# Two mixers of an adaLN block rewritten: pooling with scale, gate, shift and bias folded in, state space with dt in the exponent and GpSimd left with the masks

## The chip, the cores and the metric

The kernel runs as one launch on one core of a Trainium2 chip. The metric is device microseconds (us) of an execution. A core has a matrix engine (TensorE, PE in the profile, with its weight loads as PEld), VectorE (DVE), ScalarE (ACT), GpSimd (POOL) and SyncE (SP), whose queue issues every DMA of this kernel. The engines run their own queues in order and wait for one another through semaphores.

## The reference, cut to what matters

Two model blocks run one after the other on x of 256 tokens by 1024 channels, in fp32. The first has two layers of FFN, token mixer (gated delta rule beside attention) and FFN; the change leaves it alone. The second has a layer with a state-space mixer and a layer with a pooling mixer, each between two FFNs; a vector c gives each of its steps a shift, scale and gate, sums over `ada_w`. The state-space mixer runs over 256 context tokens first and hands its final states to the 256 main tokens; it has 32 heads in 4 groups, two directions d, chunks of 128 tokens.

```python
# state space, per direction, chunk and head; a_cum = cumsum(dt * A)
xdt = x * dt
states = einsum(B, exp(a_last - a_cum), xdt)          # per chunk
h = h * exp(a_last) + states                          # over the chunks
Lmat = exp(where(mask, a_cum[l] - a_cum[s], -inf))
y_diag = einsum(C @ B.T, Lmat, xdt); y_off = C @ h_in * exp(a_cum)
y = d_skip * x + sum over d of (y_diag + y_off)
out = rmsnorm_per_group(y * silu(z)) @ w_out          # context: only h_final is kept

# pooling, 4 groups of 256 channels, windows 2, 4, 8, 16 on a 4 x 64 grid
u = rmsnorm(x) * (1 + sc) + sh
pooled[g] = mean_over_window(u[g]) - u[g]             # a fixed 256 x 256 matrix per group
x = x + gate * scale * (pooled @ w[g] + bias)
```

## The kernel before

Tokens lie in two tiles (t = 0, 1) of 128 rows. A weight stream feeds almost all of the program: a unit is one 512 KB DMA into a `raw` buffer (6 of them), a cast to a short fp32r part `hi` on ACT (L345), the rest `lo` on DVE (L346), and three fp32r matmuls for each product (`mm3`, L351 to L353). Some units ("whole", L384 and L411) keep fp32 and show two matmul instructions a product. `stream` runs units with the loads ahead; the last five units of a phase ("deep") keep their t = 1 matmuls back, so that PE has work while tile 0 is finished and normalised for the next phase. `tick` works on the `ada_w` sums in the background: a DMA into one of two `ad` buffers (L530), a DVE multiply-add (L540), matmuls. Intermediate tiles of 128 by 512 are pages, 38 of them; PSUM has 4 banks "ps" and 4 "mm". `merge(a, b, r)` writes two pieces of work alternately, and a scheduler that runs before the launch orders each engine's queue; SP's queue issues DMAs in that order and stops at one whose buffer is not free.

Around the change the program goes: the FFN pair (main and context tokens), `ssd_ctx`, `ssd_lat`, FFN, FFN, `pool_mix`, FFN, final norm.

`ssd_ctx` projects the context (four streams us[0..3], one a group); core(g) transposes the group's tokens (L1622), copies them to SBUF (L1716), multiplies by the decay to the chunk's end and dt on POOL (`ended`, L1689), multiplies with B on PE (L1723) and stores the states (L1728). core(0..2) run beside us[1..3]; core(3) runs after them, interleaved with `mid`, the norm of the main tokens (L683, L690, transposes L248, L702, split L723/724).

`ssd_lat` has a head (z, dt and the B and C projections, 17 units), then `shared` (with `stacks`, which brings a_cum into the form that the masks take), then four core(g), merged with the streams of the other groups' projections and z. In core(g) POOL makes 8 masked stacks (L1784), PE two products that give the exponent (L1827/1828), ACT takes Exp (L1830, W), W is multiplied by dt (L1832; d = 0 on DVE, d = 1 on POOL), DVE adds the two directions (L1844) and multiplies by C B^T (L1845), and PE applies W (`diagonal`, L1792). The off-diagonal part goes L1839 (PE), L1841 and L1842 (DVE). The skip term d_skip * x is POOL's (L1816). Then the gate, the norm (L1795 to L1800), and the output units.

`PoolPrep` norms x for the pooling mixer: `scaled` (L1908), shift added (L1913), the bias added to x on POOL (L1916), with `pool_b`, `pool_scale` and the pooling matrices `poolq` loaded in `a`. `pool_mix` pools all groups (L1940), splits the result into hi and lo (`split`, L254/255), multiplies with `pool_w` as streamed units, and adds acc * scale * gate to x (L1927/1928).

## Time and profile before

| what | value |
| --- | --- |
| median of 3 runs | 3037.53 us (3035.7 to 3040.81) |
| the profiled execution | 3034.64 us, span 3032.9 us |
| PE busy | 2899.7 us (96%) |
| DVE busy | 2226.4 us (73%) |
| ACT busy | 1343.6 us (44%) |
| POOL busy | 176.0 us (6%), 148 instructions |

The profile shows one execution. The span is the time from its first to its last recorded instruction; the execution's own time is 1.7 us longer. Of the view of stretches the reader takes each engine's busy time between two moments and the clock that PE was granted (1.00 is 2.4 GHz, half of it 1.2 GHz). The chain is the sequence of work that ended last, followed back from the end: what stands on it could have shortened the run, what doesn't lay beside it. The waits say what ended an engine's idle time.

### The profile page before, as it was taken

Reading aid. Unit: us, or ns where it says so; the run is one execution under the profiler, and the core shown is the slowest. Engines: PE = TensorE matmul, PEld = TensorE weight load, DVE = VectorE, ACT = ScalarE, POOL = GpSimd, SP = SyncE. Lnnn points to the kernel's source line nnn. Section 1 sums busy time; section 2 is a strip of 40 time slices with the busy share of each in tenths; the row PEclk is TensorE's granted clock in tenths of the full one; section 3 lists DMA queues with packets and bytes.
Section 4 is the critical chain, followed back from the end, with each engine's and each line's share of the span. In section 5 each row is a group of like instructions: output and inputs, shape, how many; then the busy total and the mean of one; then the engine's idle time right before and its main releaser. Section 6 shows DMA issues by size and latency. Waiting matters only on the chain.

```text
span 3032.9 us, 42634 instructions
## 1 busy us (share of the span) xinstructions
PE 2899.7 (96%) x16035; PEld 2429.6 (80%) x16035; DVE 2226.4 (73%) x4000; ACT 1343.6 (44%) x2110; POOL 176.0 (6%) x148
## 2 busy tenths in 40 slices
PE   7998999999999899999999999998989999998898
PEld 4988776779889797678898888886866798897697
DVE  6779757777677776677878655776799875888754
ACT  4544323554444443245545223454535544543443
POOL 1000110000000011000000000002044000001000
PEclk9999999999999999999999999999999999999899
DMA  8885534468778742245776545844523587788563
GB/s 279 288 287 174 169 100 121 131 203 265 248 243 288 258 150 79 85 143 160 232 232 210 154 148 168 298 159 136 170 79 126 180 278 239 231 295 284 167 186 134
DMA packets 275777, 589.56 MB, mean 194 GB/s; under 512 B 28759, under 2 KB 72933, under 8 KB 275571
## 3 DMA queue, kind: packets, MB, share of 16 engines
q1 hardware_dynamic: 275571, 586.84, 59.7%
q8 instruction: 126, 2.06, 0.3%
q14 instruction: 80, 0.66, 0.1%
HBM read 582.57 MB, written 4.19 MB: 193 GB/s over the span
## 4 chain that ended last, share of the span: by engine, by line
PE 73%; DVE 15%; DMA 5%; ACT 4%; issue 3%; POOL 0%; SPq 0%; DVEq 0%; ACTq 0%; POOLq 0%
PE mm L351 19%; PE mm L352 18%; PE mm L353 18%; PE mm L411 5%; PE mm L384 4%; DMA ad<-ada_w 3%; DVE lo L346 2%; PE ps L248 2%; DVE acc L540 2%; PE ps L1260 1%; ACT hi L345 1%; PE ps L558 1%; PE ps L1267 1%; DMA raw<-w_branch_a 1%; PE ps L1160 1%
## 5 line engine op out<-in xcount | busy, mean ns | idle before, releaser
L345 ACT CAST hi<-raw 128x1024 fp32r<-128x1024 f32 x591 | 615.7, 1044 | 875.0 <-PE mm L352 369.8
L346 DVE TENSOR_TENSOR lo<-raw,hi 128x1024 fp32r<-128x1024 f32 x591 | 714.2, 1217 | 302.4 <-ACT hi L345 290.4
L351 PE MATMUL mm<-hTa,lo 128*128 128x256 f32 (+1 forms) x2160 | 649.5, 301 | 14.0 <-DVE lo L346 9.6
L352 PE MATMUL mm<-hTa,hi 128*128 128x256 f32 (+1 forms) x2160 | 642.6, 298 | 0.0
L353 PE MATMUL mm<-hTa,hi 128*128 128x256 f32 x1872 | 530.6, 284 | 0.0
L351 PEld LDWEIGHTS mm<-hTa,lo 128*128 128x128 f32 x2160 | 413.0, 191 | 30.5 <-DVE lo L346 10.6
L352 PEld LDWEIGHTS mm<-hTa,hi 128*128 128x128 f32 x2160 | 413.3, 191 | 13.3 <-issue 1.4
L540 DVE SCALAR_TENSOR_TENSOR acc<-ad,cond,acc 128x1024 f32<-128x1024 f32 x238 | 308.6, 1297 | 87.1 <-DMA ad<-ada_w 85.0
L353 PEld LDWEIGHTS mm<-hTa,hi 128*128 128x128 f32 x1872 | 359.0, 192 | 0.0
L351 PE MATMUL mm<-hi,pg 128*128 128x512 f32 (+1 forms) x844 | 332.6, 394 | 0.4 <-DVE pg L2014 0.4
L352 PE MATMUL mm<-hi,pg 128*128 128x512 f32 (+1 forms) x844 | 328.6, 389 | 0.0
L353 PE MATMUL mm<-lo,pg 128*128 128x512 f32 (+1 forms) x844 | 327.6, 388 | 0.0
L351 PE MATMUL mm<-hi,hTa 128*128 128x512 f32 (+1 forms) x444 | 183.4, 413 | 25.7 <-DVE hTa L724 18.0
L411 PE MATMUL mm<-hTb,raw 128*128 128x256 f32 x896 | 205.8, 384 | 0.0
L411 PEld LDWEIGHTS mm<-hTb,raw 128*128 128x128 f32 x896 | 169.8, 193 | 27.5 <-issue 5.6
L351 PEld LDWEIGHTS mm<-hi,pg 128*128 128x128 f32 x844 | 158.6, 188 | 33.9 <-issue 1.7
L352 PE MATMUL mm<-hi,hTa 128*128 128x512 f32 (+1 forms) x468 | 185.1, 396 | 0.0
L352 PEld LDWEIGHTS mm<-hi,pg 128*128 128x128 f32 x844 | 158.7, 188 | 32.8 <-issue 2.2
L353 PEld LDWEIGHTS mm<-lo,pg 128*128 128x128 f32 x844 | 158.6, 188 | 32.8 <-issue 0.5
L353 PE MATMUL mm<-lo,hTa 128*128 128x512 f32 (+1 forms) x468 | 184.8, 396 | 0.0
L384 PE MATMUL mm<-raw,hTb 128*128 128x512 f32 x320 | 151.7, 605 | 0.0
L248 PEld LDWEIGHTS ps<-con,pg 128*128 128x128 f32 x748 | 87.6, 143 | 53.6 <-issue 29.6
(443 smaller groups left out, 4510.0 us busy)
## 6 DMA issues: line engine op xcount, KB each, us to landing
ad<-ada_w SPq DMA_DIRECT2D x272, 512.0 KB
raw<-ffn_w SPq DMA_DIRECT2D x264, 512.0 KB
raw<-ffn_w_down SPq DMA_DIRECT2D x110, 512.0 KB
raw<-w_in SPq DMA_DIRECT2D x104, 512.0 KB
raw<-ffn_w_gate SPq DMA_DIRECT2D x88, 512.0 KB
raw<-ffn_w_up SPq DMA_DIRECT2D x88, 512.0 KB
raw<-ssd_w_in SPq DMA_DIRECT2D x60, 512.0 KB
raw<-w_branch_a SPq DMA_DIRECT2D x16, 512.0 KB
```

The source lines that it names most:

```text
L248: T.transpose(o[:, sl], src[:, sl], ident)
L345: in_order("hi", ACT.copy(hi[:, 0:m], raw[:, 0:m]))
L346: in_order(lane, eng.tensor_sub(lo[:, 0:m], raw[:, 0:m], hi[:, 0:m]))
L351: T.matmul(o, sl, mh, start=first, stop=False)
L352: T.matmul(o, sh, mh, start=False, stop=False)
L353: T.matmul(o, sh, ml, start=False, stop=last)
L384: T.matmul(d[c0 // 512][:, 0:min(cw, c0 + 512) - c0], sf, wt[c0 // 512], start=k == 0, stop=k == kt - 1)
L411: T.matmul(acc[m][:, 0:S], wt[0][:, SL[m]], hT.whole[:, k, :], start=k == 0, stop=k == KD - 1)
L540: after_edge(V.scalar_tensor_tensor(out=o, in0=w, scalar=sc, in1=o, op0=ALU.mult, op1=ALU.add))
L558: T.matmul(q, ones, self.acc[i][h], start=True, stop=True)
L1160: T.matmul(qs[:, col:col + 1], sq[:, hh * S + t * P:hh * S + (t + 1) * P], ones[:, 0:1], start=True, stop=True)
L1260: T.matmul(blk(y[:, H2[h]]), M[t][:, sl], odd(Ub[t][:, sl]), start=True, stop=True)
```

## The change

State space. `stacks` forms log(dt) (floored at 1e-37, ACT's Ln) and an extra accumulating matmul with the identity subtracts it from one of the two exponents, so that Exp gives W already times dt; the multiplies of L1832 go, and hi, lo and the stacks have 512 columns of source instead of 256. `ended` moves from POOL to DVE. The skip term moves to DVE, which reads x straight from the transposes' PSUM bank. The last multiply of the norm moves from DVE to ACT. `ssd_ctx` runs the norm of the main tokens within g = 2 and returns core(3), which is merged with the head of `ssd_lat`.

Pooling. `PoolPrep.early` runs in the background of the FFN before: it loads the column sums of the pooling matrices (`poolc`), bias, scale, `pool_w` and `poolq`, and folds scale * gate into `pool_w` and the bias. The shift enters the pooled product as a product of one row (shift by column sums), the bias as a product with a row of ones; x is only scaled. The pooled result is copied once and multiplied in fp32, and x takes the sum from PSUM.

```diff
         def stacks(self, t):
-            rep_ = pg()
+            rep_, lg = pg(), small(64, tag="lg")
+            V.tensor_scalar(out=lg, in0=self.dt[t], scalar1=1e-37, scalar2=None, op0=ALU.max)
+            ACT.activation(lg, lg, AF.Ln)
             for d in range(2):
                 V.tensor_copy(rep_[:, d * P:(d + 1) * P].rearrange("p (n c) -> p n c", c=HS), bcm(self.dA[t][:, d * HS:(d + 1) * HS], 4))
+                V.tensor_scalar(out=rep_[:, S + d * P:S + (d + 1) * P].rearrange("p (n c) -> p n c", c=HS), in0=bcm(lg[:, d * HS:(d + 1) * HS], 4),
+                                scalar1=-1.0, scalar2=None, op0=ALU.mult)
             q = ps()
             for d in range(2):
-                T.matmul(q[:, d * P:(d + 1) * P], rep_[:, d * P:(d + 1) * P], C("le" if d == 0 else "ge"), start=True, stop=True)
-            hl, st = pg(R32), pg(R32)
-            hi, lo = hl[:, 0:S], hl[:, S:2 * S]
-            ACT.copy(hi, q[:, 0:S])
-            V.tensor_sub(lo, q[:, 0:S], hi)
+                ra, rl, tri = rep_[:, d * P:(d + 1) * P], rep_[:, S + d * P:S + (d + 1) * P], C("le" if d == 0 else "ge")
+                T.matmul(q[:, S + d * P:S + (d + 1) * P], ra, tri, start=True, stop=True)
+                T.matmul(q[:, d * P:(d + 1) * P], ra, tri, start=True, stop=False)
+                T.matmul(q[:, d * P:(d + 1) * P], rl, ident, start=False, stop=True)
+            hi, lo, st = pg(R32), pg(R32), pg(R32)
+            ACT.copy(hi, q)
+            V.tensor_sub(lo, q, hi)
             c = lambda n: C("quad")[:, n:n + 1]
-            for o, a in ((st[:, 0:S], 0), (st[:, S:2 * S], 3)):
-                V.tensor_scalar(out=o, in0=hi, scalar1=c(a), scalar2=c(a + 2), op0=ALU.mult, op1=ALU.add)
-                V.scalar_tensor_tensor(out=o, in0=lo, scalar=c(a + 1), in1=o, op0=ALU.mult, op1=ALU.add)
+            for sl_, a in ((slice(0, S), 0), (slice(S, 2 * S), 3)):
+                V.tensor_scalar(out=st[:, sl_], in0=hi[:, sl_], scalar1=c(a), scalar2=c(a + 2), op0=ALU.mult, op1=ALU.add)
+                V.scalar_tensor_tensor(out=st[:, sl_], in0=lo[:, sl_], scalar=c(a + 1), in1=st[:, sl_], op0=ALU.mult, op1=ALU.add)
             self.left[t] = [st[:, d * P:(d + 1) * P] for d in range(2)]
             self.right[t] = [st[:, S + d * P:S + (d + 1) * P] for d in range(2)]
...
             e = pg()
-            G.tensor_mul(h8(e), h8(xt), bc(self.dx[t][:, d * HS + g * 8:d * HS + g * 8 + 8], 64))
+            V.tensor_mul(h8(e), h8(xt), bc(self.dx[t][:, d * HS + g * 8:d * HS + g * 8 + 8], 64))
             return e
...
         run(us[0])
-        for g in range(4):
+        for g in range(3):
             c = core(g)
-            if g < 3:
-                advance(us[g + 1], CN)
-                merge(us[g + 1], c, CR)
-                run(c)
-            else:
-                for _ in c:
-                    next(mid, None)
+            advance(us[g + 1], CN)
+            if g == 2:
+                run(first_of(mid, NT))
+            merge(us[g + 1], c, CR)
+            run(c)
         run(mid)
+        return core(3)
+    left_over = [None]
...
-        run(stream(zs + dt.units + conv_units(hT, 4096, 16, BT) + conv_units(hT, 4608, 20, CT)))
+        head = stream(zs + dt.units + conv_units(hT, 4096, 16, BT) + conv_units(hT, 4608, 20, CT))
+        merge(head, left_over[0], 1.0)
+        run(left_over[0])
...
                 rsqrt(rs, ss, 1.0 / 512, EPS, 1)
-                V.tensor_scalar(out=yy, in0=yy, scalar1=rs, scalar2=None, op0=ALU.mult)
+                ACT.activation(yy, yy, AF.Copy, scale=rs)
...
-                xt[t] = pg()
-                ACT.copy(xt[t], to_tok(xT[g], t))
+                xt[t], y[g, t] = pg(), pg()
+                q = to_tok(xT[g], t)
+                ACT.copy(xt[t], q)
+                V.tensor_mul(h8(y[g, t]), h8(q), bc(sc_["dsk"][:, g * 8:g * 8 + 8], 64))
                 e[t] = pg()
                 V.tensor_mul(h8(e[t]), h8(xt[t]), bc(dt.dx[t][:, hd(t)], 64))
                 yield
             masked(0, 1)
-            for t in range(NT):
-                y[g, t] = pg()
-                G.tensor_mul(h8(y[g, t]), h8(xt[t]), bc(sc_["dsk"][:, g * 8:g * 8 + 8], 64))
...
-                    h0 = d * HS + g * 8 + i * 4
-                    (G if d else V).tensor_mul(h4(W[t, i, d]), h4(W[t, i, d]), bc(dt.dt[t][:, h0:h0 + 4]))
...
     class PoolPrep(Prep):
...
+        def early(self):
+            for _ in range(4):
+                yield
+            self.q, self.w = [], []
+            self.sums, self.bias = pg(), pg()
+            for h in range(2):
+                load(self.sums[32 * h:32 * h + 1, :].rearrange("p (g l) -> p g l", l=S), A["poolc"][2 * h:2 * h + 2, :].unsqueeze(0))
+                load(self.bias[32 * h:32 * h + 1, :], A["pool_b_2"][0, 2 * h:2 * h + 2, :].rearrange("g d -> (g d)").unsqueeze(0))
+            for g in range(4):
+                self.w.append(pg())
+                load(self.w[g].rearrange("p (k d) -> p k d", k=2), A["pool_w_2"][0, g].rearrange("(k p) d -> p k d", p=P))
+            yield
+            for h in range(2):
+                psc = pg()
+                load(psc, A["pool_scale_2"][0, h * 512:(h + 1) * 512].partition_broadcast(P))
+                yield
+                V.tensor_mul(psc, psc, self.m.has("gate", 0)[:, h * 512:(h + 1) * 512])
+                V.tensor_mul(self.bias[32 * h:32 * h + 1, :], self.bias[32 * h:32 * h + 1, :], psc[32 * h:32 * h + 1, :])
+                yield
+                for g in (2 * h, 2 * h + 1):
+                    w_ = self.w[g].rearrange("p (k d) -> p k d", k=2)
+                    V.tensor_mul(w_, w_, bcm(psc[:, g % 2 * S:g % 2 * S + S], 2))
+                    yield
+            for g in range(4):
+                self.q.append(pg())
+                load(self.q[g].rearrange("p (t l) -> p t l", t=NT), A["poolq"][g].rearrange("(t p) l -> p t l", p=P))
+            yield
         def scaled(self, t, h, src, r):
-            V.scalar_tensor_tensor(out=self.xn[t, h], in0=src, scalar=r, in1=self.m.has("sc", 0)[h], op0=ALU.mult, op1=ALU.mult)
+            ins = V.scalar_tensor_tensor(out=self.xn[t, h], in0=src, scalar=r, in1=self.m.has("sc", 0)[h], op0=ALU.mult, op1=ALU.mult)
+            edge[0] = ins.ins
         def b(self, t):
-            for h in range(2):
-                u = self.xn.pop((t, h))
-                edge[0] = V.tensor_add(u, u, self.m.has("sh", 0)[h]).ins
-                self.xn["u", t, h] = u
-            for h in range(2):
-                G.tensor_add(x(t, h), x(t, h), self.rows[h][0])
+            pass
     def pool_mix(prep, m, nxt):
         yield ()
         flush()
-        u = prep.xn
+        u, sh = prep.xn, m.has("sh", 0)
         acc = Lazy(2)
...
+        row = lambda ap, h: ap[32 * h:32 * h + 1]
+        pooled, qs = [], [[(mmb if g > 1 else ps)() for _ in range(2)] for g in range(4)]
+        def pool(g, t):
             for c in range(2):
                 k = g * 2 + c
-                for t in range(NT):
-                    T.matmul(q[:, c * S:(c + 1) * S], u["u", t, k // 4][:, SL[k % 4]], qv[:, t, :], start=t == 0, stop=t == NT - 1)
-            pooled[g] = split(q)
-            us += tok_units(lambda k, t, g=g: tuple(a[:, k * S + t * P:k * S + (t + 1) * P] for a in pooled[g]), A["pool_w_2"][0, g],
-                            lambda t, g=g: [acc[t][g // 2][:, (g % 2) * S:(g % 2 + 1) * S]], (lambda t, g=g: ended(t, g // 2)) if g % 2 else None)
-        run(stream(seam(us, False)))
+                o = qs[g][c][:, 0:S]
+                if t == 0:
+                    T.matmul(o, row(sh[k // 4], k // 4)[:, SL[k % 4]], row(prep.sums, k // 4)[:, g % 2 * S:g % 2 * S + S], start=True, stop=False)
+                T.matmul(o, u[t, k // 4][:, SL[k % 4]], prep.q[g][:, t * S:t * S + S], start=False, stop=t == NT - 1)
+        for t in range(NT):
+            for g in range(4):
+                pool(g, t)
+                if t:
+                    p_ = pg()
+                    pooled.append(p_)
+                    ACT.copy(p_[:, 0:S], qs[g][0][:, 0:S])
+                    V.tensor_copy(p_[:, S:], qs[g][1][:, 0:S])
+        for t in range(NT):
+            for h in range(2):
+                o = acc[t][h]
+                T.matmul(o, row(ones, h), row(prep.bias, h), start=True, stop=False)
+                for g in (2 * h, 2 * h + 1):
+                    for k in range(2):
+                        T.matmul(o[:, g % 2 * S:g % 2 * S + S], pooled[g][:, k * S + t * P:k * S + (t + 1) * P], prep.w[g][:, k * S:k * S + S], start=False, stop=g % 2 + k == 2)
+                V.tensor_add(x(t, h), x(t, h), o)
+            nxt.a(t)
+        for t in range(NT):
+            nxt.b(t)
+        yield
...
-        mid = ahead(p0) if i + 1 == PAIR else ()
+        mid = ahead(p0) if i + 1 == PAIR else nxt.early() if keys[i + 1:i + 2] == [(1, 1, 1)] else ()
...
-            ssd_ctx(p1, ahead(preps[LAT]))
+            left_over[0] = ssd_ctx(p1, ahead(preps[LAT]))
...
+    arrays["poolc"] = POOLQ.sum(1)
```

POOL in the state-space core, group 0, before (L1784 masks, L1816 skip term, L1832 W times dt):

```order
L1784 TENSOR_TENSOR pg_20123<-pg_20064,con 128x512
L1784 TENSOR_TENSOR pg_20125<-pg_20064,con 128x512
L1784 TENSOR_TENSOR pg_20159<-pg_20064,con 128x512
L1784 TENSOR_TENSOR pg_20161<-pg_20064,con 128x512
L1816 TENSOR_TENSOR pg_20163<-pg_20131,sdsk 128x512
L1816 TENSOR_TENSOR pg_20165<-pg_20140,sdsk 128x512
L1784 TENSOR_TENSOR pg_20231<-pg_20092,con 128x512
L1784 TENSOR_TENSOR pg_20233<-pg_20092,con 128x512
L1832 TENSOR_TENSOR pg_20228<-pg_20228,pg_19581 128x512
L1784 TENSOR_TENSOR pg_20254<-pg_20092,con 128x512
L1784 TENSOR_TENSOR pg_20256<-pg_20092,con 128x512
L1832 TENSOR_TENSOR pg_20251<-pg_20251,pg_19581 128x512
```

and after (L1793 masks):

```order
L1793 TENSOR_TENSOR pg_20143<-pg_20074,con 128x512
L1793 TENSOR_TENSOR pg_20145<-pg_20074,con 128x512
L1793 TENSOR_TENSOR pg_20183<-pg_20074,con 128x512
L1793 TENSOR_TENSOR pg_20185<-pg_20074,con 128x512
L1793 TENSOR_TENSOR pg_20249<-pg_20112,con 128x512
L1793 TENSOR_TENSOR pg_20251<-pg_20112,con 128x512
L1793 TENSOR_TENSOR pg_20270<-pg_20112,con 128x512
L1793 TENSOR_TENSOR pg_20272<-pg_20112,con 128x512
```

Between the masks nothing is left.

PE where `ssd_ctx` ends and the head of `ssd_lat` begins, before (L1622 transposes of x, L1723 states, L248 transposes of the norm, L351 to L353 the head's first units):

```order
L1622 MATMUL ps_19238<-con,pg_19171 128x128 x2
L1622 MATMUL ps_19238<-con,pg_19191 128x128 x2
L1622 MATMUL ps_19267<-con,pg_19171 128x128 x2
L1622 MATMUL ps_19267<-con,pg_19191 128x128 x2
L1723 MATMUL ps_19297<-pg_19295,pg_18903 128x512
L1723 MATMUL ps_19301<-pg_19299,pg_18910 128x512
L1723 MATMUL ps_19311<-pg_19309,pg_18903 128x512
L248 MATMUL ps_19315<-con,pg_19246 128x128 x4
L248 MATMUL ps_19326<-con,pg_19248 128x128 x4
L1723 MATMUL ps_19339<-pg_19337,pg_18910 128x512
L248 MATMUL ps_19341<-con,pg_19275 128x128 x4
L248 MATMUL ps_19352<-con,pg_19277 128x128 x4
```

and after (L1729 is the states' matmul):

```order
L1729 MATMUL ps_19255<-pg_19253,pg_18903 128x512
L1729 MATMUL ps_19259<-pg_19257,pg_18910 128x512
L1729 MATMUL ps_19269<-pg_19267,pg_18903 128x512
L1729 MATMUL ps_19273<-pg_19271,pg_18910 128x512
L248 MATMUL ps_19283<-con,pg_19145 128x128 x4
L248 MATMUL ps_19294<-con,pg_19147 128x128 x4
L248 MATMUL ps_19305<-con,pg_19167 128x128 x4
L248 MATMUL ps_19316<-con,pg_19169 128x128 x4
L1622 MATMUL ps_19341<-con,pg_19215 128x128 x2
L1622 MATMUL ps_19341<-con,pg_19235 128x128 x2
L351 MATMUL mm_19333<-hi_19329,hTa_19281 128x512
L352 MATMUL mm_19333<-hi_19329,hTa_19281 128x512
```

The states of core(3) no longer stand between the last projection and the head's first matmul; its transposes, and later its states, come between the head's units.

SP at the end of the FFN before the pooling mixer, before:

```order
L325 DMA raw_25427<-ffn_w_down 128x1024
L530 DMA ad_25344<-ada_w 128x1024
L325 DMA raw_25443<-ffn_w_down 128x1024
L530 DMA ad_25359<-ada_w 128x1024
L530 DMA ad_25374<-ada_w 128x1024
L325 DMA raw_25474<-ffn_w_down 128x1024
L325 DMA raw_25664<-pool_w 128x2x256
```

and after (L1923 loads the pooling matrices):

```order
L1923 DMA pg_25406<-poolq 128x2x256
L530 DMA ad_25387<-ada_w 128x1024
L1923 DMA pg_25408<-poolq 128x2x256
L530 DMA ad_25403<-ada_w 128x1024
L1923 DMA pg_25410<-poolq 128x2x256
L1923 DMA pg_25412<-poolq 128x2x256
L325 DMA raw_25414<-ffn_w_down 128x1024
L530 DMA ad_25430<-ada_w 128x1024
L325 DMA raw_25433<-ffn_w_down 128x1024
L325 DMA raw_25449<-ffn_w_down 128x1024
L325 DMA raw_25465<-ffn_w_down 128x1024
L325 DMA raw_25496<-ffn_w_down 128x1024
```

The pool's loads, which came after the last `ffn_w_down`, now stand ahead of the last five, with five more loads of `ada_w`.

## Rows read from the trace of the kernel before

**Rows 1.** The page, busy time by engine.
```profile
PE 2899.7 (96%) x16035; PEld 2429.6 (80%) x16035; DVE 2226.4 (73%) x4000; ACT 1343.6 (44%) x2110; POOL 176.0 (6%) x148
```

**Rows 2.** Stretches: length, busy PE, PEld, DVE, ACT, POOL, clock, DMA share, GB/s.
```profile
2060.40:2107.00 46.60, 43.20 (x192) 34.24 (x191) 26.38 (x47) 20.10 (x39) 14.21 (x11) 0.96 0.50 151
2107.00:2129.40 22.40, 14.05 (x41) 6.32 (x39) 20.50 (x53) 10.73 (x26) 5.47 (x6) 0.85 0.18 62
2129.40:2204.00 74.60, 72.97 (x445) 65.00 (x446) 55.43 (x133) 42.51 (x75) 0.00 (x0) 1.00 0.55 178
2204.00:2365.00 161.00, 144.52 (x606) 100.02 (x605) 149.52 (x266) 73.28 (x133) 76.16 (x56) 0.98 0.31 100
...
2700.00:2794.00 94.00, 91.09 (x508) 78.43 (x506) 77.68 (x89) 39.27 (x52) 4.73 (x4) 1.00 0.91 312
2794.00:2831.00 37.00, 18.05 (x90) 15.38 (x89) 29.55 (x58) 10.52 (x23) 7.15 (x5) 0.78 0.22 72
```

**Rows 3.** PE's waits, end of the context: engine, line, releaser: us, times, longest.
```profile
PE ps L1723 <- POOL pg L1689: 4.3, 2, 3.4
```

**Rows 4.** Chain, context's end: start, us, what.
```profile
2084.72 0.87 PE ps L1622 x8
...
2090.77 1.72 PE ps L1723 x4
...
2108.66 0.40 DVE pg L1614
```

**Rows 5.** PE's waits in the state-space core.
```profile
PE ps L1792 <- DVE pg L1845: 5.5, 4, 2.8
```

**Rows 6.** Groups of the core, by form: busy us, mean ns | idle before, releaser.
```profile
L1784 POOL TENSOR_TENSOR pg<-pg,con 128x512 fp32r<-128x512 f32 x32 | 41.5, 1318 | 87.0 <-issue 83.4 <-PE ps L1819 2.8 <-DVE pg L1844 0.8
...
L1832 POOL TENSOR_TENSOR pg<-pg,pg 128x512 f32<-128x512 f32 x16 | 24.0, 1500 | 70.9 <-ACT pg L1830 70.9
...
L1842 DVE TENSOR_TENSOR pg<-pg,pg 128x512 f32<-128x512 f32 x16 | 17.1, 1070 | 0.5 <-DVE pg L1841 0.5
...
L1845 DVE TENSOR_TENSOR pg<-pg,pg 128x512 f32<-128x512 f32 x16 | 16.2, 1012 | 0.0
...
L1844 DVE TENSOR_TENSOR pg<-pg,pg 128x512 f32<-128x512 f32 x16 | 15.2, 951 | 0.5 <-POOL pg L1832 0.5
L1832 DVE TENSOR_TENSOR pg<-pg,pg 128x512 f32<-128x512 f32 x16 | 13.4, 839 | 4.6 <-ACT pg L1830 4.6
...
L1816 POOL TENSOR_TENSOR pg<-pg,sdsk 128x512 f32<-128x512 f32 x8 | 11.2, 1418 | 4.9 <-ACT pg L1809 4.9
...
L1830 ACT ACT_TABLE_LOAD x6 | 7.7, 1283 | 0.1
...
L1800 DVE TENSOR_SCALAR pg<-pg,yrs 128x512 f32<-128x512 f32 x6 | 2.9, 480 | 0.0
```

**Rows 7.** DVE in the core: start, us, line, operation.
```profile
2225.80 0.69 DVE L1842 TENSOR_TENSOR pg<-pg,pg 128x512 f32<-128x512 f32 x1 [0.47 <-DVE pg L1841]
...
2230.48 0.68 DVE L1841 TENSOR_TENSOR pg<-ps,pg 128x512 f32<-128x512 f32 x1
...
2231.92 1.52 DVE L1842 TENSOR_TENSOR pg<-pg,pg 128x512 f32<-128x512 f32 x1
```

**Rows 8.** Chain, pooling mixer.
```profile
2796.71 3.34 DVE pg L1913 x2
...
2806.82 1.68 DVE pg L1913
2808.55 6.91 PE ps L1940 x24
...
2819.20 0.65 DVE xres L1928
...
2822.37 1.13 DVE lo L346
```

**Rows 9.** SP's queue before the pooling mixer: start, us, queue, line.
```profile
2768.03 0.37 SPq L325 DMA_DIRECT2D raw<-ffn_w_down  x1
...
2780.99 2.67 SPq L1897 DMA_DIRECT2D pg<-poolq  x4
```

More of the change, by code (lines that the diff above doesn't have):

```diff
@@ L1915, in b @@
-            for h in range(2):
-                G.tensor_add(x(t, h), x(t, h), self.rows[h][0])
+            pass
     def pool_mix(prep, m, nxt):
@@ L1920, in pool_mix @@
         flush()
-        u = prep.xn
+        u, sh = prep.xn, m.has("sh", 0)
         acc = Lazy(2)
-        us = []
-        def ended(t, h):
-            tmp = pg()
-            V.tensor_mul(tmp, acc[t][h], prep.rows[h][1])
-            V.tensor_add(x(t, h), x(t, h), tmp)
-            if h:
-                nxt.a(t)
-                defer(4 - 2 * t, lambda: nxt.b(t))
-        pooled = {}
-        for g in range(4):
-            qv = prep.q[g].rearrange("p (t l) -> p t l", t=NT)
-            q = ps()
+        row = lambda ap, h: ap[32 * h:32 * h + 1]
```

14 lines of the change are left out of this document (removed).

## The prediction

> **What bounds the kernel now.** I read the busy shares first, then the view of stretches around the two mixers, then PE's waits in each of them, and last the chain and SP's queue. The page shows PE busy for 96% of the span [rows 1], so over most of the program only fewer matmuls would help, and the change takes none of weight away. What it can win lies where PE stands idle. The stretches show how much that is: 46.6 − 43.2 = 3.4 us at the end of the context, 22.4 − 14.05 = 8.4 us between the last context projection and the main tokens' first matmul, 1.6 us in the head, 161.0 − 144.5 = 16.5 us in the state-space core, 37.0 − 18.05 = 19 us between the last matmul before pooling and the next FFN's first [rows 2]. Together 49 us, 1.6% of the span, and these are the whole prize, but for a few microseconds lost to a lower clock (0.78 in the pooling stretch, 0.85 at the context's end [rows 2]).
>
> Each stretch has another limit. At the context's end PE waits once for 3.4 us on POOL's multiply [rows 3], and afterwards on a chain of DVE instructions. In the core DVE is busy 149.5 of 161 us [rows 2], and the longest of PE's waits is for the last DVE step of W [rows 5]. In the pooling stretch it is a chain through DVE, PE and DVE again [rows 8]. The head, and the FFNs around pooling, are PE's own.
>
> **The change part by part.** The sum is made against the profiled execution, 3034.64 us, which is 2.9 us under the median of 3037.53.
>
> *Context and head.* `ended` on DVE ends the 3.4 us wait for POOL: −3.4. The 16 multiplies then cost DVE about 0.69 each [rows 7], 11 us, spread over a stretch and a head in which it is busy 26.4 of 46.6 and 55.4 of 74.6 us [rows 2]: hidden. In the tail of 22.4 us, core(3) and the norm's sums leave; what stays is one activation (1 us), the 16 convolution steps at 0.40 [rows 4], six DVE operations at 0.6 and two transposes' rounds with the split (2.5): 1 + 6.4 + 3.6 + 2.5 = 13.5 to 14.4. I take 14.4, so −8. If the norm's transposes needn't wait behind the convolution steps, it would be 6 us less again; if core(2)'s states, which now stand ahead of them on PE, come late by a DVE queue, up to 5 more. Core(3)'s PE work comes back in the head: 8 matmul instructions at 0.43 and 16 transposes at 0.108 [rows 4] make 5.2, unhidden, since PE is full there. `stacks` has four more matmuls a tile, some 2 us in all. Net −3.4 − 8 + 5.2 + 2 = −4; ends −12 and +4.
>
> *State-space core.* DVE loses 16 multiplies by dt (13.4) and the norm's last multiply (2.9) [rows 6]. It gains 8 skip terms with an input in PSUM, 0.68 each as L1841 [rows 7], 5.4, and about 2 for log(dt) and the wider stacks. Then there is the interference. A DVE operation on two SBUF tiles takes 0.69 alone and 1.52 while POOL runs; one with an input in PSUM keeps 0.68 beside POOL [rows 7]. Over the core L1842, L1844 and L1845 at 1070, 951 and 1012 ns [rows 6] against 690 lose 6.1 + 4.2 + 5.2 = 15.5 us, and with the other forms about 25 (an estimate from their means). POOL is busy 76.2 us [rows 2], of which L1832 and L1816 are 35.2 [rows 6], 46%; so some 11 us of the stretching go with them. DVE falls to 149.5 − 13.4 − 2.9 + 5.4 + 2 − 11 = 130. PE's 144.5 is then the larger: the stage cannot fall under some 146, a gain of at most 15 to 16, and 2 more where the clock was low. POOL also leaves the chain of W, where d = 1 took 1500 ns. I do not take the whole: W's first DVE step still follows Exp, and the stack's chain at the start is longer by a Ln with its table load (1283 ns [rows 6]) and by wider operations, by 2 to 4 us, partly beside filling projections. I take −10; ends −18 and 0. ACT has seven more table loads, 7 x 1.28 = 9 us, and 8 scalings of 0.6, beside 73 of 161 busy [rows 2]: nothing, as long as Exp isn't behind them.
>
> *What the skill says of the interference.* The Trainium skill (SBUF — State Buffer, "Who interferes with whom") has VectorE and GpSimd share a port pair as an exclusive lock, where the loser waits fully, for VectorE instructions with two SBUF inputs against GpSimd instructions that read SBUF. The trace agrees for this pair: 1.52 against 0.68 [rows 7]. By this rule the skip term from PSUM is free of it, and the 32 masks, which stay, still block DVE; what that would make of the time is the first rival, worked out there from rows.
>
> *Pooling.* Between the last matmul before and the first after lie 37 us [rows 2]. The additions of the shift go from the chain, 3.34 for the first tile and 1.68 for the second [rows 8]: −5.0; the 8 one-row products that replace them are 0.9. Only tile 1's 16 pooled instructions remain behind tile 1's norm, out of 24 in 6.91 (0.29 each [rows 8]): −2.3. In their place come 4 PSUM copies in two engines (1) and, for tile 0, fp32 products, 2 halves of 2 instructions at 0.43 and 8 at half of that [rows 4], 2 x 2.6 = 5.2, against the 1.5 us of the streamed units at their end: +3.7 + 1. The final DVE steps shrink from 2.6 to 1.3 (L1928 is 0.65 [rows 8]): −1.3. The residual subtraction of a weight (1.13) and the issue gaps around it inside tile 0's norm [rows 8] are earlier, since the next FFN's units no longer wait behind `pool_w`: −3. That makes −7.
>
> Against this stands the FFN ahead. DMA is at 0.91 there with 312 GB/s [rows 2]. The last `ffn_w_down` was issued at 2768.0, 26 us before the last matmul at 2794, and the pooling matrices only at 2781.0 [rows 9, 2]. Now 2.5 MB of pool data and five loads of `ada_w` (2.6 MB) stand ahead of the last five `ffn_w_down`: 5 MB / 312 GB/s = 16 us, so issue at 2784. Of the remaining 10 us, the casts take 2.3 (1.04 on ACT and 1.22 on DVE, the means of the page's largest groups) and the kept-back matmuls 5, landing 4 to 5: 1 to 2 us late. I take +2, ends −2 and +9. Net of pooling −5; ends −11 and +4. The DMAs that come later, the next FFN's gate and up weights, are issued earlier than before.
>
> Sum: −4 − 10 − 5 = −19, so 3034.6 − 19 = 3015.6 for a run like the profiled one and, with 2.9, **3018 us** for the median.
>
> **The rivals.**
>
> *The masks keep the interference (chance 0.13).* There are 32 masks of 1318 ns [rows 6], each able to stretch one DVE operation by 1.52 − 0.69 = 0.83: 27 us, as much as there is now. Then POOL's other work only took its turn with them, and none of the 11 us goes except what L1832 itself lost. DVE falls by 9 only, and at the same share (10 of 19.5) the core gains 5. Total −14: 3024. For it: DVE fills its queue, so any mask meets an operation. Against it: the masks can run early, and POOL is idle 87 us before them [rows 6].
>
> *PE becomes full (0.18).* The core comes down to PE's 146 and its low-clock spots vanish (−17), the context gives −7, pooling −9: −33, 3004. For it: all of PE's idle time in the core is ended by DVE, and DVE would have 15 us in hand. Against it: the waits for L1845 [rows 5] come at the ends of chains inside a step, which need not shrink with the busy time.
>
> *SP's queue stops in the FFN before pooling.* The 10 pages of pool data are wanted while the FFN still holds its own and those of the deep units, out of 38; before, `poolq` waited until 2781.0 [rows 9], just after that FFN's first tile was done. A DMA on SP that waits for a page holds every `ffn_w_down` behind it. There are three such places, `pool_w`, `pool_scale`, `poolq`. A stop that empties the raw buffers costs the pool's megabyte (3.4 us at 312 GB/s), a weight (1.7), its landing (2) and its casts (2.3), 9.4 us of PE. Two stops: −4 − 10 − 7 + 19 = −2, 3035, no change that can be told (chance 0.12). Three: +7, **3045, slower than before (0.08)**. It decides from a delay of 21 us on. For it: PE is full there and has nothing else. Against it: SP's order places the pool's loads between `ffn_w_down` loads, not all in one place, and pages come free with each unit.
>
> **How the numbers follow.** Forecast 0.49, masks 0.13, full PE 0.18, two stops 0.12, three 0.08. About 0.2%, 6 us, is what a measurement can tell: faster is under 3031.4. The first three make 0.80 faster, the fourth 0.12, the last 0.08. The forecast's own range is 3009 to 3027; for 8 times in 10 it must take in most of the full-PE case and the two stops: 3001 to 3035.
>
> **What would show it.** In the profile after: POOL busy about 42 us in the core and no line but the masks; L1842, L1844, L1845 at 750 to 850 ns (rival one: still about 1000); DVE near 130 and PE idle about 6 in a core of 151 us. The tail at the context's end 14 us with no wait for POOL, and a head of about 82. Pooling 30 to 32 us, with the last matmul before it 2 us later against the FFN's start. The forecast is wrong if DVE still bounds the core, if PE waits for `ffn_w_down` in the FFN before pooling, or if Ln's and Exp's table loads show up as PE's wait.

## The result and the profile after

The changed kernel takes 3006.97 us, the median of four runs (3003.21 to 3013.99), against 3038.88 us of the kernel before: ratio 0.9894, 95% interval 0.988 to 0.9909, 28 to 36 us less. A second set of runs gave 3010.91 against 3041.95, ratio 0.9894 (0.9873 to 0.9915). The profiled execution of the changed kernel was the slowest of its four, 3013.99 us with a span of 3012.2; that of before, 3034.64 us, was shorter than all four of the others. So the two profiles differ by 20.7 us where the medians differ by 32. In two more profiles, one of each kernel, the program reached the first context copy, before any changed code, at 2030.5 and 2036.4 us (2032.4 and 2036.7 in the first two): single executions scatter by some microseconds, and lengths of stages are compared below, not times of day.

Stages, each from one event to the next (first context copy on ACT, first matmul of the head, first matmul of `stacks`, last diagonal products, first matmul of the FFN, last matmul before pooling, first matmul of the next FFN, end). The second line of each kernel is its second profile.

| us | context | head | core | out | two FFN phases | pooling | rest |
| --- | --- | --- | --- | --- | --- | --- | --- |
| before | 97.0 | 72.0 | 163.4 | 33.5 | 395.6 | 37.1 | 201.9 |
| | 98.0 | 73.1 | 165.7 | 33.5 | 399.7 | 37.2 | 202.5 |
| after | 87.6 | 76.4 | 147.1 | 32.2 | 400.1 | 31.1 | 201.1 |
| | 87.6 | 76.8 | 147.2 | 32.2 | 397.8 | 30.9 | 201.0 |
| state space alone | 87.9 | 76.5 | 147.2 | 32.2 | 396.8 | 37.1 | 202.5 |
| pooling alone | 95.5 | 72.4 | 166.5 | 33.5 | 398.4 | 31.5 | 201.4 |

With the means of the lines that share the code, context to out falls from 368.0 to 343.6 us, −24.4; pooling −6.0; the rest −1.1. Together −31.5, which is what the medians show. The FFN phases scatter by 2 to 4 us in either kernel and show no difference that holds.

The stretches of the changed kernel that answer to [rows 2], columns as there: context, head, core, the FFN before pooling, pooling.

```profile
2036.70:2124.30 87.60, 78.47 (x361) 61.27 (x359) 60.59 (x153) 42.76 (x83) 0.00 (x0) 0.96 0.42 128
2124.30:2200.70 76.40, 74.74 (x441) 64.89 (x441) 58.03 (x138) 46.85 (x80) 0.00 (x0) 1.00 0.53 174
...
2200.70:2347.80 147.10, 142.99 (x635) 101.14 (x636) 127.92 (x263) 85.51 (x146) 37.11 (x32) 1.00 0.38 116
...
2685.00:2780.00 95.00, 89.09 (x471) 74.36 (x469) 74.50 (x87) 36.32 (x45) 0.00 (x0) 0.98 0.85 298
2780.00:2811.10 31.10, 25.46 (x97) 17.91 (x97) 19.07 (x63) 8.31 (x22) 0.00 (x0) 0.88 0.18 65
```

The core of before between the same two events, in its first profile and, below it, in its second:

```profile
2201.40:2364.80 163.40, 146.92 (x622) 102.20 (x622) 150.94 (x270) 75.19 (x136) 76.16 (x56) 0.98 0.32 100
```
```profile
2201.60:2367.30 165.70, 151.38 (x622) 104.86 (x622) 150.06 (x270) 75.34 (x136) 74.89 (x56) 0.95 0.32 99
```

DVE went from 150 to 128 busy us, GpSimd from 76 to 37, and PE idles 4.1 instead of 14 to 17 us. PE's clock is read beside it: in the three profiles with the old core it is 0.98, 0.95 and 0.94, in the three with the new one 1.00. At 0.95 PE is busy 151 us with the work that takes 147 at 0.98, with nearly the same waits. So the gain in the core is 16 to 19 us; on the means it is 18, of which 11 are idle time and 7 are PE's busy time (143.0 after). What set the clock isn't shown.

The groups of the core that answer to [rows 6], changed kernel (L1848 was L1842, L1850 was L1844, L1851 was L1845, L1847 was L1841; L1820 is the skip term):

```profile
L1793 POOL TENSOR_TENSOR pg<-pg,con 128x512 fp32r<-128x512 f32 x32 | 37.1, 1171 | 956.1 <-DVE pg L1673 866.0 <-ACT pg L1608 24.3 <-PE ps L1827 16.5
...
L1848 DVE TENSOR_TENSOR pg<-pg,pg 128x512 f32<-128x512 f32 x16 | 12.3, 766 | 0.1
L1850 DVE TENSOR_TENSOR pg<-pg,pg 128x512 f32<-128x512 f32 x16 | 12.2, 765 | 5.6 <-ACT pg L1838 5.4
...
L1851 DVE TENSOR_TENSOR pg<-pg,pg 128x512 f32<-128x512 f32 x16 | 11.1, 696 | 0.0
L1847 DVE TENSOR_TENSOR pg<-ps,pg 128x512 f32<-128x512 f32 x16 | 10.9, 681 | 3.5 <-PE ps L1845 3.5
...
L1820 DVE TENSOR_TENSOR pg<-ps,sdsk 128x512 f32<-128x512 f32 x8 | 5.4, 681 | 0.7 <-ACT pg L1819 0.7
```

The three forms with two SBUF inputs fell from 1070, 951 and 1012 to 766, 765 and 696 ns; the one with a PSUM input stayed at 681, and the skip term has the same price. PE's waits in the core, which were 16.4 us, all for DVE, are down to these and two of 0.2 and 0.3 us; none is for an Exp or a table load on ACT:

```profile
PE ps L1835 <- DVE pg L1701: 1.7, 1, 1.7
PE ps L1827 <- DVE rt L223: 0.8, 1, 0.8
PE ps L1845 <- DVE pg L1847: 0.8, 1, 0.8
```

The chain through pooling, changed kernel, which answers to [rows 8] (L1947 pooled products, L1960 bias, L1963 products with `pool_w`):

```profile
2784.20 0.76 DVE pg L1927
...
2785.01 3.78 PE ps L1947 x8
2788.79 2.36 PE mm L1947 x8
2791.15 1.73 PE ps L1947 x8
2792.88 1.73 PE mm L1947 x8
2794.61 1.05 PE mm L1960 x2
2795.66 1.93 PE mm L1963 x8
...
2806.54 0.70 DVE xres L1964
```

From 2785 on PE has no gap until the last product: the chain runs through PE, where before it ran through DVE's additions and the units' hi and lo. The first eight products, behind a wait of 1.9 us, take 0.47 each at a granted clock of 0.50, the last sixteen 0.22 at 1.00: the engine runs here at 1.2 GHz first and at 2.4 GHz later (0.88 granted over the stretch).

PE's waits in the context of the changed kernel, which answer to [rows 3]:

```profile
PE ps L1729 <- ACT pg L1616: 6.6, 1, 6.6
...
PE ps L1729 <- DVE pg L1695: 0.6, 2, 0.5
```

The wait for `ended` (now L1695) is down to 0.6 us. The longest is for the last projection's Silu (L1616), which comes when DVE has done the 16 convolution steps.

### The profile page after: what moved, and what is told of

It is laid out like the page before. It is cut to its first block, busy times and chain, and to the rows that moved or that the text cites. A ratio compares the mean times of both kernels' runs of the same rounds, so it can differ in the third digit from the quotient of the medians.

```text
span 3012.2 us, 42589 instructions
## 1 busy us (share of the span) xinstructions
PE 2908.4 (97%) x16059; PEld 2432.2 (81%) x16059; DVE 2190.8 (73%) x4002; ACT 1356.9 (45%) x2123; POOL 105.5 (4%) x100
## 4 chain that ended last, share of the span: by engine, by line
PE 72%; DVE 16%; DMA 6%; ACT 3%; issue 3%; SPq 0%; DVEq 0%; ACTq 0%
PE mm L351 18%; PE mm L352 17%; PE mm L353 17%; PE mm L411 5%; PE mm L384 4%; DVE lo L346 3%; DMA ad<-ada_w 3%; PE ps L248 3%; DVE acc L540 2%; PE ps L1260 1%; ACT hi L345 1%; PE ps L1267 1%; PE ps L558 1%; DMA raw<-ffn_w_down 1%; DVE pg L1611 1%
## 5 line engine op out<-in xcount | busy, mean ns | idle before, releaser
L346 DVE TENSOR_TENSOR lo<-raw,hi 128x1024 fp32r<-128x1024 f32 x587 | 710.9, 1219 | 304.9 <-ACT hi L345 295.1
L351 PE MATMUL mm<-hTa,lo 128*128 128x256 f32 (+1 forms) x2160 | 650.8, 302 | 17.6 <-DVE lo L346 9.6
L353 PE MATMUL mm<-hTa,hi 128*128 128x256 f32 x1872 | 531.6, 284 | 0.0
L351 PEld LDWEIGHTS mm<-hTa,lo 128*128 128x128 f32 x2160 | 414.1, 192 | 34.4 <-DVE lo L346 10.5
L352 PEld LDWEIGHTS mm<-hTa,hi 128*128 128x128 f32 x2160 | 414.4, 192 | 13.4 <-issue 1.4
L353 PEld LDWEIGHTS mm<-hTa,hi 128*128 128x128 f32 x1872 | 360.1, 192 | 0.0
L351 PE MATMUL mm<-hi,pg 128*128 128x512 f32 x828 | 329.5, 398 | 1.6 <-DVE pg L844 0.9
L353 PE MATMUL mm<-lo,pg 128*128 128x512 f32 x828 | 324.1, 392 | 2.7 <-DVE lo L346 2.5
L352 PE MATMUL mm<-hi,pg 128*128 128x512 f32 x828 | 323.6, 391 | 0.0
L351 PE MATMUL mm<-hi,hTa 128*128 128x512 f32 (+1 forms) x444 | 182.8, 412 | 23.0 <-DVE hTa L724 11.7
L351 PEld LDWEIGHTS mm<-hi,pg 128*128 128x128 f32 x828 | 156.0, 188 | 36.2 <-issue 2.2
L353 PEld LDWEIGHTS mm<-lo,pg 128*128 128x128 f32 x828 | 155.7, 188 | 36.4 <-DVE lo L346 4.2
L353 PE MATMUL mm<-lo,hTa 128*128 128x512 f32 (+1 forms) x468 | 184.1, 394 | 0.0
L340 DVE TENSOR_TENSOR pg<-raw,pg 128x512 fp32r<-128x512 f32 x202 | 128.8, 683 | 4.9 <-ACT pg L339 3.4
```

What stands on the lines that cost most here:

```text
L340: in_order(lane, eng.tensor_sub(lo[j], r, hi[j]))
L346: in_order(lane, eng.tensor_sub(lo[:, 0:m], raw[:, 0:m], hi[:, 0:m]))
L351: T.matmul(o, sl, mh, start=first, stop=False)
L352: T.matmul(o, sh, mh, start=False, stop=False)
L353: T.matmul(o, sh, ml, start=False, stop=last)
```

## The experiments

The first four expectations have letters of their own. For the core there are three theories: A, DVE's load was the bound and PE is now; B, the stretching of DVE by GpSimd was what PE paid for; C, the multiply in the chain of W was. The lengths of stages are of one profile each; the old core alone spreads from 163.4 to 166.5 us over three profiles.

**The halves.** Before plus the state-space edits alone; before plus the pooling edits alone; the changed kernel and the kernel before once more for a second profile. No edit but the change's own.

> The state-space half of the change alone, pooling as before. Theory A (the two halves are independent, and the profiles' stage lengths are the truth): from the context's first projection to the first matmul of the next FFN the stretch is 22 to 24 us shorter than before, everything behind it as before, the time 22 to 26 us under the kernel before. Theory B (the profiled execution of the changed kernel was a poor one, and the FFN before pooling lost time in it by chance): the same here, and pooling alone must then give 8 to 10 us. If the state-space half gives 30 us or more by the medians, the pooling half gives nothing.

> The pooling half alone, state space as before. Theory A: the stretch from the last matmul before pooling to the next FFN's first is about 31 us instead of 37, but the FFN in front of it ends 3 to 4 us later, because the pool's loads stand ahead of the last five down-projection weights: net 2 to 3 us under the kernel before, at the edge of what can be told. Theory B: the later end of that FFN was chance: net 6 to 9 us.

> The changed kernel once more, for a second profile. The unchanged first 2030 us took 4.3 us longer in the profiled run of the changed kernel than in that of the kernel before. If that is variation from one execution to the next, it differs here, and the stages behind it keep their lengths within about 1 us: core 144 to 146, context and head 163 to 165, pooling 31. The median 30 to 33 us under the kernel before.

> The kernel before once more, for a second profile: the length of its unchanged first part against the first profile (2032.4 us to the context's first copy) shows how much of a difference of two profiles is variation. Core 160 to 162, pooling 36 to 38.

State space alone: 3014.63 against 3041.95 us, ratio 0.9904 (0.9883 to 0.9925). Pooling alone: 3040.86, ratio 0.9983 (0.9969 to 0.9998), 0.6 to 9.4 us less. The kernel before against itself: 0.9994 (0.998 to 1.0008). The halves add up by stages (table above); by the medians they give 27.3 and 1.1, and the interval of the second is too wide to tell. The second profiles have longer cores than expected, 147.2 for 144 to 146 and 165.7 for 160 to 162. The later end of the FFN before pooling can't be told from the lengths: 396 to 400 us with and without the pool's early loads. That its weights come later is seen, though: over the last 95 us of that FFN ACT's casts wait for `ffn_w_down` 20 to 28 us in the three profiles with the early loads and 2 to 6 in those without, and PE waits for DVE's `lo` (L346) 2.5, 4.0 and 2.1 us against 0, 0.7 and 0.

**The multiply by dt back, on both engines and on DVE.** `stacks` is as before, without log(dt); the second run has `V` for both directions.

```diff
+            hl, st = pg(R32), pg(R32)
+            hi, lo = hl[:, 0:S], hl[:, S:2 * S]
...
                     ACT.activation(W[t, i, d], q, AF.Exp)
+                    h0 = d * HS + g * 8 + i * 4
+                    (G if d else V).tensor_mul(h4(W[t, i, d]), h4(W[t, i, d]), bc(dt.dt[t][:, h0:h0 + 4]))
```

> The changed kernel with the multiplies of W by dt put back (16 on DVE, 16 on GpSimd) and log(dt) out of the exponent; skip term, norm multiply, context and pooling stay changed. Theory A (DVE's load: the core got short because DVE fell from 149 to 129 busy us and PE, 143, became the bound): DVE rises by 16 x 0.69 and what 16 more GpSimd operations stretch, to 143 to 150; the core is 152 to 158 us from the first stack's matmul to the last diagonal instead of 145 to 148, with PE's clock under 1.00 again. Theory B (the stretching of DVE by GpSimd was most of it): GpSimd busy 37 to 61, about half of the way back, 152. Theory C (the multiply in the chain of W was what PE waited for): all of it back, 160 or more, with waits of PE for the last step of W.

> As the run before, but all 32 multiplies by dt on DVE, so that GpSimd keeps the 32 masks alone. Theory A: DVE 129 + 32 x 0.69 = 151 with no more stretching than now; the core 153 to 160. Theory B: only clean DVE work is added, GpSimd busy stays 37; the core stays under 150. Theory C: as with both engines, less 0.8 a step where GpSimd's multiply was the slower one: 155 to 158.

The core is 162.0 us with both engines and 158.4 with DVE alone, against 147.1. The times are 3031.88 us (3019.49 to 3037.19, profiled at 3020.88), ratio to before 0.9955 (0.9939 to 0.9972), and 3022.90, 0.9935 (0.9916 to 0.9955). DVE's busy time is 144.6 and 147.6: the run with more DVE work is the shorter one, and the one in which GpSimd has nothing but masks. In it the forms with two SBUF inputs take 733 to 789 ns, in the other 931 to 1006. Theory B's lengths, 152 and under 150, failed; 162.0 is what C expected, 158.4 lies in A's range and 0.4 above C's. So taking log(dt) out of the exponent gives back 11 to 15 us of the core's gain, and it is not DVE's sum alone that sets the length. The multiplies are steps in the chain of W too, so these two runs can't part C from DVE's load; the runs with products that nobody reads can.

**Masks twice.**

```diff
                     G.tensor_mul(h4(gb[t, i, d]), bcm(dt.right[t][d], 4), bc(C("pick")[:, h0:h0 + 4]))
+                    G.tensor_mul(h4(dump[0]), bcm(dt.right[t][d], 4), bc(C("pick")[:, h0:h0 + 4]))
```

> The changed kernel with every mask computed a second time on GpSimd into a page that nobody reads: 32 more operations of 1.2 us that nothing waits for. What they do, they do through the interference. Theory A: DVE's busy time rises by 32 x 0.3 to 0.83 = 10 to 27 us to 139 to 156; as long as it stays under PE's 143 the core is longer by 0 to 4 us. Theory B: the core comes back by 8 us or more. Theory C: nothing at all, under 1 us.

The core is 169.6 us, longer than before the change; 3033.45 us, ratio to before 0.9972 (0.9956 to 0.9988). The order of the instructions on PE, DVE and ACT is that of the changed kernel; GpSimd's queue alone differs. The copies hardly wait, and 23 of them stand in one row there:

```profile
2219.33 2.21 POOL L1795 TENSOR_TENSOR pg<-pg,con 128x512 fp32r<-128x512 f32 x2
2221.51 28.78 POOL L1796 TENSOR_TENSOR pg<-pg,con 128x512 fp32r<-128x512 f32 x23
2250.24 2.48 POOL L1795 TENSOR_TENSOR pg<-pg,con 128x512 fp32r<-128x512 f32 x2
```

That does two things, and PE's waits tell them apart. The next real masks came 29 us later, and PE waits 4.9 us for one of them. But its longest wait, 13.0 us, is for DVE:

```profile
2234.70 2.43 DVE L1614 SCALAR_TENSOR_TENSOR pg<-pg,sconv,pg 128x254 f32<-128x254 f32 x2
2237.06 1.52 DVE L1700 TENSOR_TENSOR pg<-pg,pg 128x512 f32<-128x512 f32 x1
2238.50 1.26 DVE L1614 SCALAR_TENSOR_TENSOR pg<-pg,sconv,pg 128x254 f32<-128x254 f32 x1
2239.68 0.68 DVE L1701 TENSOR_TENSOR pg<-pg,ps 128x512 f32<-128x512 f32 x1
```
```profile
2240.41 0.80 PE L1838 MATMUL ps<-rounded,roundedi 128*128 128x512 f32 x1 [13.03 <-DVE pg L1701]
```

Beside the row DVE has no gap, and its convolution steps, with their inputs in SBUF, follow one another every 1.18 us, where in the changed kernel it is every 0.40 with no mask beside them. DVE's busy time rises by 19.0 us (to 146.9), within theory A's range, but the core by 22.5, where A had 0 to 4 and C nothing: that is B. The next but one is the form with shorter rows.

**The skip term on GpSimd.**

```diff
-                V.tensor_mul(h8(y[g, t]), h8(q), bc(sc_["dsk"][:, g * 8:g * 8 + 8], 64))
+                G.tensor_mul(h8(y[g, t]), h8(xt[t]), bc(sc_["dsk"][:, g * 8:g * 8 + 8], 64))
```

> The changed kernel with the 8 multiplies of the skip term on GpSimd, from the SBUF copy, as before. DVE loses 8 x 0.68 = 5.4 us and gets some stretching back, up to 8 x 0.83 = 6.6. Theory A: PE is full either way, the core within 1 us. Theory B: 3 to 4 us longer. Theory C: within 1 us.

3016.29 us, core 154.2: seven longer, where A and C said under 1 and B 3 to 4. DVE is busy only 2.8 us more (130.7). GpSimd's masks now wait behind a skip term that waits for the transposes, and come six in a row beside DVE's start of a group; L1700, the first step of the state there, takes 1123 ns for 680. How the 7 us divide between the late masks and that stretching isn't settled.

**W on GpSimd for nobody.**

```diff
                     ACT.activation(W[t, i, d], q, AF.Exp)
+                    if d:
+                        h0 = d * HS + g * 8 + i * 4
+                        G.tensor_mul(h4(dump[0]), h4(W[t, i, d]), bc(dt.dt[t][:, h0:h0 + 4]))
```

> The changed kernel with 16 more GpSimd operations in the core: after each Exp of direction 1 GpSimd multiplies W by dt as before the change, but into a page that nobody reads, and W is used as it is. Nothing waits for the product; what the 16 operations do, they do by stretching DVE and by standing ahead of masks in GpSimd's queue. Theory A (PE full, DVE with 19 us to spare): DVE's two-input operations are stretched again, but the core is at most 3 us longer than 147.2. Theory B (the stretching is what PE paid for): 6 to 10 us longer, half or more of what dt_back cost (15), with PE's clock under 1.00. Theory C (only the wait for the product counted): under 1 us.

The core is 159.1 us, +12.0, at a clock of 0.99; 3018.91 us, ratio to before 0.993 (0.991 to 0.995). No instruction reads the products. The order of the other queues is almost that of the changed kernel: all of ACT's 131 instructions, 259 of DVE's 261, 628 of PE's 636. PE is idle 13.4 us instead of 4.1, and of its waits 12.2 us are for DVE, 0.7 for a mask:

```profile
PE ps L1829 <- DVE rt L223: 3.6, 1, 3.6
PE ps L1803 <- DVE pg L1852: 3.5, 1, 3.5
...
PE ps L1838 <- POOL pg L1795: 0.7, 1, 0.7
```

DVE's forms, with the same work as in the changed kernel (L1853 is L1848 there, L1855 L1850, L1856 L1851, L1852 L1847):

```profile
L1856 DVE TENSOR_TENSOR pg<-pg,pg 128x512 f32<-128x512 f32 x16 | 16.3, 1019 | 0.0
L1853 DVE TENSOR_TENSOR pg<-pg,pg 128x512 f32<-128x512 f32 x16 | 15.9, 992 | 0.1
L1855 DVE TENSOR_TENSOR pg<-pg,pg 128x512 f32<-128x512 f32 x16 | 14.6, 911 | 4.1 <-ACT pg L1840 4.0
L1852 DVE TENSOR_TENSOR pg<-ps,pg 128x512 f32<-128x512 f32 x16 | 10.9, 681 | 4.8 <-PE ps L1850 4.8
```

DVE's busy time rises by 12.1 us (127.9 to 140.0) and the core by 12.0. Sixteen GpSimd operations that nobody needs cost 12 us, where the real multiplies on both engines cost 14.9. That is theory B's mechanism, and more than its 6 to 10; A (at most 3) and C (under 1) fail. DVE has 19 us to spare in both cores, of 147 and of 159, and PE pays all the same. The costs don't add: clean multiplies on DVE alone cost 11.3, so how the gain divides between less work and less stretching isn't shown.

**The context's end as before.** `ssd_ctx` with core(3) and the norm after the last projection, as in the kernel before, `ended` staying on DVE.

```diff
-        for g in range(3):
+        for g in range(4):
             c = core(g)
-            advance(us[g + 1], CN)
-            if g == 2:
-                run(first_of(mid, NT))
-            merge(us[g + 1], c, CR)
-            run(c)
+            if g < 3:
+                advance(us[g + 1], CN)
+                merge(us[g + 1], c, CR)
+                run(c)
+            else:
+                for _ in c:
+                    next(mid, None)
         run(mid)
-        return core(3)
+        return iter(())
```

> The changed kernel with the end of the context as before: core(3) and the norm of the main tokens after the last projection, nothing left over for the head. By the forecast's own terms the stretch from the context's first copy to the head's first matmul is 87.6 + 8 = 96 us, the head 76.5 - 5 = 71.5, together 3 us longer than the changed kernel's 164. If core(3) beside the head cost nothing, the head stays near 76 and the two are 8 us longer; if moving it gave nothing, they are unchanged.

Context 98.2, head 71.9, together 170.1 against 164.0; 3013.88 us. So the new order takes 10.6 us from the context (8 in the expectation) and gives 4.5 back in the head (5), 6.1 net for an expected 3. But 98.2 is no shorter than before (97.0, 98.0, 95.5): in the old order `ended` on DVE gave nothing. PE's waits in that stretch:

```profile
PE ps L1729 <- DVE pg L1695: 6.6, 4, 5.4
PE ps L1729 <- DVE rt L223: 3.4, 1, 3.4
PE mm L351 <- DVE hTa L724: 1.1, 1, 1.1
```

The wait for GpSimd [rows 3] became one for the same product on DVE (L1695), where it stands behind convolution steps and among the norm's. The new order with `ended` on GpSimd wasn't tried.

**The norm first.** The last projection's convolution steps are written after the main tokens' norm, and the rest of core(2) is left over too.

```diff
-        us = [stream(conv_units(hT, 2048 + g * 512, g * 4, xT[g], True)) for g in range(4)]
+        us = [stream(conv_units(hT, 2048 + g * 512, g * 4, xT[g], True, late if g == 3 else None)) for g in range(4)]
...
-            run(c)
+            if g < 2:
+                run(c)
         run(mid)
-        return core(3)
+        for taps in late:
+            taps()
+        return chained(c, core(3))
```

> A try at a faster version: in the changed kernel the head's first matmul waits for the transposes of the main tokens' norm, which stand behind the 16 convolution steps of the last context projection on DVE and behind four state matmuls on PE. Here the last projection's convolution steps are written after the norm, and what is left of core(2) goes to the head as well. The context's stretch is 4 to 6 us shorter than 87.6, the head up to 2 us longer, since core(2)'s matmuls move into it and PE is full there; the time 2 to 5 us under the changed kernel's. If DVE's queue in the head becomes the wait instead, the head takes all of it back.

Context 78.8, head 93.1: 8.8 us won and 16.7 lost; 3019.34 us (3006.28, the profiled one, to 3024.57), ratio to before 0.9925 (0.9903 to 0.9947). PE's waits in the head:

```profile
PE ps L1663 <- DVE pg L1661: 6.4, 2, 4.8
PE mm L351 <- ACT pg L339: 1.7, 1, 1.7
PE mm L351 <- DVE hTa L724: 1.1, 1, 1.1
```

The work moved into DVE's queue in the head makes dt late (L1661). PE idles 10.2 us of the head instead of 1.7, and at a clock of 0.91 instead of 1.00 it is busy 82.9 us instead of 74.7. The last branch of the expectation holds: the head takes all of it back, and more.

**The bias on x.** Full rows of the scaled bias, added to x on DVE while PE pools; the products with the row of ones go.

```diff
-                load(self.bias[32 * h:32 * h + 1, :], A["pool_b_2"][0, 2 * h:2 * h + 2, :].rearrange("g d -> (g d)").unsqueeze(0))
+                load(self.bias[h], A["pool_b_2"][0].rearrange("g d -> (g d)")[h * 512:(h + 1) * 512].partition_broadcast(P))
...
                     V.tensor_copy(p_[:, S:], qs[g][1][:, 0:S])
+                    V.tensor_add(x(g // 2, g % 2), x(g // 2, g % 2), prep.bias[g % 2])
...
-                T.matmul(o, row(ones, h), row(prep.bias, h), start=True, stop=False)
```

> A try at a faster version of the pooling half: in the profile of the changed kernel PE is busy without a gap from the first pooled product to the last product with pool_w, and four products of the bias with a row of ones cost it 1.05 us each. Here the scaled bias is loaded as full rows and added to x on DVE while PE pools, and the four products go. If PE is what sets that stretch, it is 4.2 us shorter, 27 us instead of 31, and the time 4 us under the changed kernel's. If the stretch is set by DVE (the copies and the norm between the products), the four additions of 0.6 to 0.7 us take part of it back: 28.5 to 31. It is slower, 32 or more, only if the two additions that stand between the norms of tile 0 and tile 1 delay tile 1's.

Pooling takes 27.1 us, 4 less than with the change. The products now run through:

```profile
2789.03 1.89 PE L1947 MATMUL mm<-pg,pg 128*128 128x256 f32 x8
2790.76 7.07 PE L1963 MATMUL mm<-pg,pg 128*128 128x256 f32 x32
2799.48 1.09 PE L248 MATMUL ps<-con,pg 128*128 128x128 f32 x8 [1.65 <-DVE pg L690]
```

3004.74 us (3003.31 to 3007.69), ratio to before 0.9878 (0.9857 to 0.9899). It is the fastest kernel of this study and beats the one before; that it beats the changed one is shown by the stage, not by the medians, whose intervals overlap.

## Why the prediction was right, and where it was short

Sign and range held (3007 in 3001 to 3035), but the forecast of 3018 gave −19 to −21 where −32 came: the second rival's mechanism, given 0.18 and 3004, is nearer.

*Context and head, forecast −4:* measured −5.0 on the means of the table (169.3 to 164.3, with the lines that share the code). But the forecast counts 2 us for `stacks` here, which by the table's boundaries lie in the core: without them it is −6. The parts: the tail −10.6 for a forecast of −8, the head +4.5 for 5.2. The −3.4 for `ended` failed: in the old order the product is as late on DVE.

*Core, forecast −10, ends −18 and 0:* −16 to −19, the mis-sized term. DVE's busy time came out at 128 for a forecast of 130. More of the stretching went than foreseen: the three forms of [rows 6] lost 15.5 us to it before and lose 2.5 now, where the forecast had 11 us for all forms. The step that failed is "I do not take the whole": a gain of 10 was taken for 20 us less on DVE, for fear that chains inside a step need not shrink. They did: PE's waits for L1845, which were held against the second rival, have no counterpart in the changed core, and PE idles 4.1 us. The picture of two sums of which the larger bounds the stage was too simple as well, for DVE's time counts even where it is the smaller sum:

| core | DVE busy | GpSimd busy | length |
| --- | --- | --- | --- |
| changed | 127.9 | 37.1 | 147.1 |
| + 16 unread products | 140.0 | 67.1 | 159.1 |
| + 32 unread masks | 146.9 | 74.3 | 169.6 |
| skip term on GpSimd | 130.7 | 50.7 | 154.2 |
| dt back, both engines | 144.6 | 64.6 | 162.0 |
| dt back, DVE | 147.6 | 45.0 | 158.4 |
| before | 150.9 | 76.2 | 163.4 |

In the two runs that add nothing but GpSimd work, the core grows by as much as DVE's busy time or more: 12.0 for 12.1 and 22.5 for 19.0, with 4.9 of the latter spent on a late mask. Clean DVE work cost less, 11.3 us for 19.7. The skip term's run (7 for 2.8) fits no such line. And PE's clock, which I had at 2 us, went with 4 to 9 us of PE's busy time (146.9, 151.4 and 151.6 to 143.0).

*The masks keep the interference:* wrong in size. Thirty-two masks alone leave the three forms at 696 to 766 ns. By the times in the trace 14 of the 32 masks fall where DVE has no 128x512 operation on two SBUF tiles; before the change that held for 9 of GpSimd's 56 operations. The Trainium skill (SBUF — State Buffer, "Who interferes with whom") says that a VectorE instruction with two SBUF inputs contends with a GpSimd instruction that reads SBUF, and that one with at most one SBUF input, outside the two-port modes, does not. The unread products agree, 766 to 992 ns with two SBUF inputs and 681 unchanged with one in PSUM, and so does the skip term from PSUM, 681.

*Pooling, forecast −7 and +2 before it:* −6.0, but not by the forecast's sum. That has no term for the bias's four products with a row of ones, 4 x 1.05 = 4.2 us on the chain, which the run with the bias on x bears out (−4.0), and it leaves its own 0.9 out (those products lie beside the norm, off the chain). The rest gave −10 where the sum has −7: up to the end of the last product −5.0 for −2.6 (27.3 to 26.5 us with the bias's 4.2), and from there to the next FFN's first matmul −5.2 for −4.3 (9.8 to 4.6). That the total came near is luck. The +2 can't be told from the scatter of the FFN phases, 395.6 to 400.1; its cause, weights that come later, is seen. SP's queue did not stop for pages in any profile long enough to be seen in these lengths. The price of such a stop has 2 us for a landing, where the trace of before has 4.7 from the issue at 2768.03 [rows 9] to the cast that waits for that weight.

*Not in the forecast:* −1.3 in the output units and −1.1 after pooling. By the table the first comes with the state-space half, the second with the pooling half; which edit gave them wasn't tried.

## What to carry to other kernels

An instruction on GpSimd that nobody waits for is not free where DVE is on PE's path: ask what DVE reads beside it. Arithmetic that can be put into an exponent leaves both engines at once, and an operation with an input in PSUM kept its 0.68 us on DVE whatever GpSimd did. Before moving work out of a waiting engine's way, look at what stands ahead of it in the queue it goes to: `ended` on DVE only changed the name of the wait, and the norm put first lost more behind DVE's queue than it won.

## What was not expected of the hardware

Sixteen GpSimd multiplies, 30 us more of its busy time, beside a DVE with 19 us to spare made the core 12 us longer. A row of 23 GpSimd operations tripled the time of DVE's convolution steps, 0.40 to 1.18 us. And two profiles of one kernel differ by 2.3 us in a stage of 164: with nearly the same waits PE is busy 4.5 us longer at a granted clock of 0.95 than at 0.98.
